# The scan of the RWKV heads: one series of batches over all four head pairs instead of four series

## The chip, the cores and the metric

One core of a Trainium2 chip. Times are device microseconds (us) of one launch; lower is better. The kernel before took a median of 2058.11 us in 3 runs (2053.48 to 2059.82).

## The reference, cut to what matters

The kernel is a two-layer trunk over 512 latent tokens and 256 context tokens of width 1024. In the even layer half of the heads are RWKV-7 heads, scanned forwards and backwards over the tokens:

```python
def rwkv7_scan(f, d, s0, reverse):
    def step(state, inp):
        r_t, w_t, k_t, v_t, kk_t, a_t = inp
        sa = jnp.einsum('bhvk,bhk->bhv', state, -kk_t)
        state = (state * w_t[:, :, None, :] + sa[..., None] * (kk_t * a_t)[:, :, None, :]
                 + v_t[..., None] * k_t[:, :, None, :])
        return state, jnp.einsum('bhvk,bhk->bhv', state, r_t)
...
    _, yl_f = rwkv7_scan(fl, 0, s_cf, False)
    _, yl_b = rwkv7_scan(fl, 1, s_cb, True)
    out_lat = rwkv7_output(fl, yl_f + yl_b, prm, pa_lat.dtype)
```

`rwkv7_prepare` computes r, k, v, the decay w, the rate a and the normalised key kk; `rwkv7_output` normalises y by head, adds a bonus term and gates it. The rest of the trunk (attention, MLP, adaLN modulation) isn't changed.

## The kernel before, in words

The eight RWKV heads are four pairs; a pair fills the 128 partitions. Tokens are cut into 12 chunks of 64 for each direction, and three chunks (`NB`) make a batch, so a pair has four batches.

**The prep** of a pair (`prep`) has four parts, with marks between them. Up to FRONT it makes the normalised key, the decays and rates (`wide` tiles at L405, L415, L865). Up to READY it makes the factors AR, BK and the chunk matrices XI (L903 to L948; L917 multiplies them on PE, L918 masks them on VectorE). The matrices then go through DRAM (`nscr`, L925 and L928) into another layout, N. Up to MERGE VectorE inverts the 32x32 blocks in 31 steps of two instructions (L954, L955), and the result goes back through DRAM (`xscr`, `tscr`, L959 to L967) into XI and `xw`. Behind MERGE the blocks are merged into 64x64 inverses: L974 and L982, two `wide` tiles each.

**The scan** of a pair (`chunks`) has seven stages for a batch: `factors` (transposes), `masked`, `own`, `solved` (multiplies by XI, L1077), `local` (L1089), `passed` (L1015) and three `step`s, which carry the state from chunk to chunk. Each batch's last stages are interleaved with the next batch's first ones, within one pair: a pair begins and ends with stages that have no partner. `mix_out` finishes a pair's output y.

**Who is handed out when.** These are Python generators; the trace is the order in which they are advanced. For each pair the main loop (L1488 to L1551) takes one stage of the scan a turn, 37 turns in all, and after each turn advances a background generator `behind` by 1.8 yields (RATE3) and the modulation matmuls `ada` (L353) by 0.7 (RATE4). `behind` deals in turn from the next pair's prep up to MERGE, the previous pair's `mix_out`, and the prep of the pair after the next up to FRONT. When the scan of the pair is through, `rest` hands out what is left: the prep of the pair after the next up to READY, then the next pair's merge. Only then does the next pair's scan begin.

The Tile planner orders each engine's instructions from this trace: what is traced earlier has precedence. Almost every matmul stage of the scan, the prep and `mix_out` writes a tile from `wide()`, of which there are two (two PSUM banks each); `py`, `pd` and the modulation's tile are others, one buffer each. AR, BK, XI, `wc` and `kds` of even and odd pairs lie in two pools, one buffer each, so a pair's prep from FRONT on waits for the scan of the pair two before it; `kds` also for that pair's `mix_out` (L1190). SyncE (SP) issues nearly all transfers, in order, the modulation weights (L341, three buffers of 512 KB) among them.

Of the kernel before, what the change touches and what calls it, by code (L numbers as in the profile page):

```python
# [174 lines left out]
def trunk(ctx: ExitStack, tc: tile.TileContext, xT, cT, vec_d, wada, we, wo_in, wout, wf1, wf2, lw2_d, la2_d, lg2_d,  # L175
# [5 lines left out]
    def act(o, i, f=AF.Copy, **k):  # L181
        return S.activation(o, i, f, **k)  # L182

    def pool(name, bufs=1, **k):
        return tc.tile_pool(name=name, bufs=bufs, reuse_waits="tile", **k)
# [657 lines left out]
    def prep(p, R, rt, iv, sts, res):  # L843
# [102 lines left out]
            yield QUIET  # L946
        G.tensor_tensor(kds, kds, kd, op=ALU.add)
        stt(kds, kds, VV["rk"][:, p:p + 1], r, op0=ALU.mult, op1=ALU.mult)  # L948
        yield READY
        for s in range(31):  # L950
            a, b = s + 1, 31 - s
# [10 lines left out]
        for d in range(2):  # L962
# [2 lines left out]
                i0 = d * 48 + b * 24  # L965
                nc.sync.dma_start(xv[o:o + 32, :, 32 * b:32 * b + 32], xscr[p, i0:i0 + 24].rearrange("i s t -> s i t"))
            nc.sync.dma_start(w1[d * 64:d * 64 + 32].rearrange("s (i t) -> s i t", t=32), tscr[p, d * 48:d * 48 + 24].rearrange("i s t -> s i t"))  # L967
        res[p] = (AR, BK, XI, wc, kds)
        yield MERGE
        for q in range(2):  # L970
            pw = one()
# [14 lines left out]

    NB = 3

    def chunks(p, y, ct, pch, res):

# [5 lines left out]
        ch = (FWD, BWD)  # L998
        v = ct.tile([128, T], F32, name="v")
        nc.sync.dma_start(v, scr[3 + 3 * p + 2])  # L1000
        py = pch.tile([128, 2, 512], F32, name="py")
        pd = pch.tile([128, 128], F32, name="pd")
        yp = py[:, :, 0:384].rearrange("p h (c f) -> p h c f", f=64)
        B = [{} for _ in range(NCH // NB)]
        last = None
        env = {}
# [55 lines left out]
        def own(b):  # L1062

            AK, Z, XA = (B[b][x] for x in ("AK", "Z", "XA"))
            px = wide()[:, 0:NB * 128].rearrange("p (i h v) -> p i h v", i=NB, h=2)
            for i in range(NB):
                for h, d in HD:
                    PE.matmul(px[half(d), i, h], AK[half(1 - d), h, i], Z[half(1 - d), i, d, h], start=True, stop=True)
            act(XA[:, :, :, 0:64], px)
# [12 lines left out]
        def local(b):  # L1082

            BT, Z = B[b]["BT"], B[b]["Z"]
            pn = wide()[:, 0:NB * 128].rearrange("p (i d v) -> p i d v", i=NB, d=2)
            for i in range(NB):
                for d in range(2):
                    for h in range(2):
                        PE.matmul(pn[half(h), i, d], BT[:, h, d * NB + i, 0:64], Z[:, i, d, h], start=True, stop=True)  # L1089
            N = B[b]["N"] = ct.tile([128, NB, 2, 64], F32, name="Nb", bufs=2)  # L1090
            act(N, pn)
            for i in range(NB):
                for h in range(2):
                    for d in range(2):
                        c = ch[d][NB * b + i]
                        first = not b and not i
                        o, x, y_ = yp[half(c % 2), h, c // 2], BT[:, h, d * NB + i, 64:128], Z[:, i, d, h]
                        if first:
                            env["y"] = PE.matmul(o, x, y_, start=True, stop=False)
                        else:  # L1100
                            with tc.issue_after(env["y"].ins):
                                PE.matmul(o, x, y_, start=False, stop=False)
# [17 lines left out]
        def step(b, i):  # L1120
            nonlocal X
            s = NB * b + i
            N = B[b]["N"][:, i]
            if not s:
                X = N
                return
            MQ, St = B[b]["MQ"], X
            if s < NCH - 1:
                for d in range(2):
                    for h in range(2):  # L1130
                        PE.matmul(pd[half(h), half(d)], MQ[half(h), d, i, 0:64], St[half(h), d], start=True, stop=True)
                X = ct.tile([128, 2, 64], F32, name="x", bufs=2)
                tt(X, pd.rearrange("p (d v) -> p d v", d=2), N, op=ALU.add)
            for d in range(2):
                c = ch[d][s]
                for h in range(2):
                    with tc.issue_after(env["y"].ins):
                        PE.matmul(yp[half(c % 2), h, c // 2], MQ[half(h), d, i, 64:128], St[half(h), d], start=False, stop=s == NCH - 1)

        nb = NCH // NB  # L1140
        for b in range(nb + 1):
            if b < nb:
                factors(b)
                yield
            if b:
                local(b - 1)
                yield
            if b < nb:
                masked(b)
                yield  # L1150
            if b:
                passed(b - 1)
                yield
            if b < nb:
                own(b)
                yield
            if b:
                step(b - 1, 0)
                yield
            if b < nb:  # L1160
                solved(b)
                yield
            if b:
                for i in range(1, NB):
                    step(b - 1, i)
                    yield
        act(y.rearrange("p c (h f) -> p h c f", h=2), yp)
        yield

    def centred(y):  # L1170

# [99 lines left out]
    def until(g, mark):  # L1271
        for t in g:
            if t == mark:
                return
            yield t

    def front(p):

        if p < 4:
            preps[p] = prep(p, R, rt, iv, sts, res)  # L1280
            yield from until(preps[p], FRONT)
# [188 lines left out]
    with ExitStack() as p2:  # L1470
# [10 lines left out]
            if t != QUIET:  # L1481
                next(ag, None)
        gate = mix_gate(tl)
        for t in until(preps[1], READY):
            next(ag, None)
        for t in preps[0]:
            next(ag, None)
        for p in range(4):  # L1488
            cg, n = chunks(p, y, ct, pch, res), 0

            def turns(*gs):
                gs = list(gs)
                while gs:
                    for g in list(gs):
                        t = next(g, gs)
                        if t is gs:
                            gs.remove(g)
                        else:
                            yield t

            def behind():
                def out():
                    return mix_out(p - 1, y, gate, tl, res) if p else iter(())
                if p < 3:
                    yield from turns(until(preps[p + 1], MERGE), out(), front(p + 2))
                else:
                    yield from out()
                    for x in mixs[::-1]:
                        x.close()
                    p3w["W"] = ffstream(p3w["x"].enter_context(pool("wp3")), 0)  # L1510
                    m0 = p3w["m0"] = p3w["m"].enter_context(pool("m0"))
                    p3w["last"] = m0.tile([128, T], F32, name="last")
                    yield from bonus(3, tl, res, gate, p3w["last"])
                    mh = m0.tile([128, KT, 256], F32R, name="mh")
                    ml = m0.tile([128, KT, 256], F32R, name="ml")
                    p3w["mh"] = mh, ml
                    for j in range(8):
                        for _ in range(3):
                            yield
                        p3w["W"].ahead(j + 1)  # L1520
                        if j in (5, 6):
                            a, b = ((4, 8), (0, 3))[j - 5]
                            if a:
                                mr = m0.tile([128, 4, 256], F32, name="mr")
                            else:
                                mr = tl.tile([128, T], F32, name="t", bufs=2).rearrange("p (k t) -> p k t", k=3)
                            nc.sync.dma_start(mr, mixd[a:b, :, 0:256].rearrange("k p t -> p k t"))
                            split(mh[:, a:b], ml[:, a:b], mr)
            bg = behind()
            due = [0.0, 0.0]  # L1530
            t = None
            for _ in cg:
                n += 1
                due[0] += RATE3
                due[1] += RATE4
                while due[0] >= 1:
                    due[0] -= 1
                    next(bg, None)
                while due[1] >= 1:
                    due[1] -= 1  # L1540
                    next(ag, None)
            def rest():
                if p < 2:
                    yield from until(preps[p + 2], READY)
                if p < 3:
                    yield from preps[p + 1]
            for t in itertools.chain(bg, rest()):
                due[1] += RATE5
                while due[1] >= 1:
                    due[1] -= 1  # L1550
                    next(ag, None)  # L1551
        for _ in ag:
            pass
        end = mix_last(3, y, tl, p3w["last"], p3w["gate"], mk)
# [336 lines left out]
```

## Time and profile before

| | us |
|---|---|
| profiled execution | 2055.19 |
| its span | 2053.4 |
| PE matmul busy | 1932.7 (94% of the span) |
| PE weight load busy | 1633.5 (80%) |
| VectorE busy | 1124.7 (55%) |
| ScalarE busy | 817.0 (40%) |
| GpSimd busy | 122.2 (6%) |
| mean granted clock of TensorE | 0.971 of full speed |

In the chain of waits that ended last PE has 63% of the span, VectorE 7%, ScalarE 3%, DMA 2%. A stretch of the trace is given from the start of the span. In rows of instructions the columns are: start, length in us, engine, line and operation, written tile and read tiles, shape, how many; in brackets the engine's idle time just before and what ended it. A name like PE L1077 means the instruction of line 1077 on that engine. A matmul in full 32-bit precision shows as two records.

### The profile page before, as it was taken

The numbers are of one execution on the slowest core, as the hardware profiler recorded it, in microseconds if no ns is written. First come the engines' busy times: TensorE is split into PE (matmuls) and PEld (weight loads), VectorE is DVE, ScalarE is ACT, GpSimd is POOL, SyncE is SP. The second block draws the span as 40 slices with busy tenths as digits, with TensorE's granted clock in tenths as the row PEclk, the third lists the DMA queues.
The fourth block names the chain that finished last, engine by engine and source line by source line (L and its number), as shares of the span: only waits on it lengthen the run. The fifth ranks groups of instructions, "written<-read, shape, count | busy, mean of one in ns | idle before, by whom it ended". The sixth has DMA issues, their size and how long they took to land.

```text
span 2053.4 us, 38620 instructions
## 1 busy us (share of the span) xinstructions
PE 1932.7 (94%) x16412; PEld 1633.5 (80%) x16412; DVE 1124.7 (55%) x1999; ACT 817.0 (40%) x1531; POOL 122.2 (6%) x149
## 2 busy tenths in 40 slices
PE   6999988988888899999999999899999899999997
PEld 3878767666666897888888889898888798888887
DVE  6576477547464377233433345856575575444445
ACT  3466442534335244311322122435686645222332
POOL 1000011011100000000000000001021000000000
PEclk9999989999999999999999999999999999999998
DMA  7422334666634233211221021342111334322221
GB/s 309 149 65 78 108 109 129 209 195 207 207 126 145 71 112 132 73 61 42 83 72 62 32 83 42 103 151 68 51 39 37 123 102 166 102 83 82 97 88 42
DMA packets 112013, 217.47 MB, mean 106 GB/s; under 512 B 38496, under 2 KB 63968, under 8 KB 111328
## 3 DMA queue, kind: packets, MB, share of 16 engines
q1 hardware_dynamic: 96544, 191.66, 28.6%
q10 hardware_dynamic: 15296, 23.33, 3.2%
q8 instruction: 129, 2.11, 0.4%
q14 instruction: 44, 0.36, 0.1%
HBM read 184.29 MB, written 28.05 MB: 103 GB/s over the span
## 4 chain that ended last, share of the span: by engine, by line
PE 63%; DVE 7%; ACT 3%; issue 3%; DMA 2%; POOL 1%; POOLq 0%; ACTq 0%; DVEq 0%; SPq 0%
PE x L1588 45%; PE x L430 5%; PE ax L530 2%; PE ax L511 2%; PE b L1015 1%; PE b L493 1%; PE ad L353 1%; PE b L1077 1%; PE b L494 1%; DMA w_raw<-in_wada_dram 1%; DVE X L955 1%; DVE nacc L288 1%; ACT Z L182 1%; DVE pr L954 1%; POOL r L264 0%
## 5 line engine op out<-in xcount | busy, mean ns | idle before, releaser
L182 ACT ACTIVATE w_hi<-w_raw 128x1024 fp32r<-128x1024 f32 x183 | 192.3, 1058 | 484.1 <-PE x L1588 369.1
L225 DVE TENSOR_TENSOR w_lo<-w_raw,w_hi 128x1024 fp32r<-128x1024 f32 x181 | 220.8, 1223 | 194.6 <-ACT w_hi L182 193.0
L1588 PE MATMUL x<-fl,w_hi 128*128 128x256 f32 (+1 forms) x864 | 290.9, 338 | 3.9 <-DVE fl L1675 3.9
L1588 PE MATMUL x<-uh,w_hi 128*128 128x512 f32 (+1 forms) x864 | 286.7, 337 | 3.0 <-ACT uh L182 3.0
L1588 PE MATMUL x<-fh,w_lo 128*128 128x256 f32 (+1 forms) x864 | 289.4, 336 | 0.0
L1588 PE MATMUL x<-ul,w_hi 128*128 128x512 f32 (+1 forms) x864 | 287.9, 336 | 0.0
L1588 PE MATMUL x<-uh,w_lo 128*128 128x512 f32 (+1 forms) x864 | 287.6, 336 | 0.0
L1588 PE MATMUL x<-fh,w_hi 128*128 128x256 f32 (+1 forms) x864 | 286.9, 337 | 0.0
L1602 DVE TENSOR_TENSOR oa<-x,oa 128x512 f32<-128x512 f32 (+1 forms) x184 | 103.1, 563 | 207.9 <-PE x L1588 207.0
L430 PE MATMUL x<-uh,w_hi 128*128 128x256 f32 (+1 forms) x560 | 190.2, 340 | 1.6 <-ACT po L182 1.3
L430 PE MATMUL x<-uh,w_lo 128*128 128x256 f32 (+1 forms) x560 | 189.1, 338 | 0.0
L430 PE MATMUL x<-ul,w_hi 128*128 128x256 f32 (+1 forms) x560 | 188.5, 337 | 0.0
L1588 PEld LDWEIGHTS x<-fl,w_hi 128*128 128x128 f32 x864 | 164.3, 190 | 22.0 <-DVE fl L1675 4.3
L1588 PEld LDWEIGHTS x<-uh,w_hi 128*128 128x128 f32 x864 | 161.8, 189 | 21.1 <-ACT uh L182 3.9
L1588 PEld LDWEIGHTS x<-fh,w_lo 128*128 128x128 f32 x864 | 164.1, 190 | 17.9
L1588 PEld LDWEIGHTS x<-fh,w_hi 128*128 128x128 f32 x864 | 162.1, 190 | 20.0 <-ACT fh L182 2.5
L1588 PEld LDWEIGHTS x<-ul,w_hi 128*128 128x128 f32 x864 | 162.8, 189 | 17.7
L1588 PEld LDWEIGHTS x<-uh,w_lo 128*128 128x128 f32 x864 | 162.8, 189 | 17.6
L430 PEld LDWEIGHTS x<-uh,w_hi 128*128 128x128 f32 x560 | 107.5, 192 | 12.5 <-issue 2.7
L430 PEld LDWEIGHTS x<-uh,w_lo 128*128 128x128 f32 x560 | 107.7, 192 | 9.4 <-issue 1.2
L430 PEld LDWEIGHTS x<-ul,w_hi 128*128 128x128 f32 x560 | 107.8, 192 | 9.2 <-issue 1.3
L1674 DVE TENSOR_TENSOR rl<-rl 128x512 f32<-128x512 f32 (+1 forms) x108 | 59.3, 550 | 77.7 <-ACT fh L182 77.5
(304 smaller groups left out, 3398.7 us busy)
## 6 DMA issues: line engine op xcount, KB each, us to landing
w_raw<-in_wf_dram SPq DMA_DIRECT2D x128, 512.0 KB
w_raw<-in_wada_dram SPq DMA_DIRECT2D x96, 512.0 KB
w_raw<-in_we_dram SPq DMA_DIRECT2D x21, 512.0 KB
w_raw<-in_wo_in_dram SPq DMA_DIRECT2D x18, 512.0 KB
w_raw<-in_wout_dram SPq DMA_DIRECT2D x16, 512.0 KB
hsc<-h ACTq DMA_DIRECT2D x8, 1024.0 KB
scr<-po ACTq DMA_DIRECT2D x21, 384.0 KB
h<-hsc SPq DMA_DIRECT2D x7, 1024.0 KB
```

Source lines behind the costliest of these rows:

```text
L182: return S.activation(o, i, f, **k)
L225: eng.tensor_tensor(o_lo, x, o_hi.bitcast(F32), op=ALU.subtract)
L288: V.tensor_reduce(acc, sq.rearrange("p k t -> p t k"), axis=AX.X, op=ALU.add)
L353: PE.matmul(ps[o:o + 32, 0:256], si[:, 2 * kp + k, :], w[:, k, j * 256:(j + 1) * 256], start=kp == 0, stop=kp == 3)
L430: PE.matmul(ps[:, 0:b - a], x, y, start=j == 0, stop=j == len(pairs) - 1)
L493: PE.matmul(ps[:, off:off + n], qs, kh, start=True, stop=False)
L494: PE.matmul(ps[:, off:off + n], qs, kl, start=False, stop=True)
L511: PE.transpose(pt[:, (kb - k0) * 128:(kb - k0 + 1) * 128], P[:, kb * 128:(kb + 1) * 128], ident)
L530: PE.matmul(po[h * 64:h * 64 + 64, 0:128], v(h, k), pts[h][:, k], start=k == 0, stop=k == n - 1)
L1588: PE.matmul(o, a, b, start=n == 0, stop=n == len(pairs) - 1)
L1602: tt(oa[:, m, tok], ps, oa[:, m, tok], op=ALU.add)
L1674: tt(r, r, r, op=ALU.mult)
```

## The change

The four scans become one. `chunks` is split: `stages` holds the stages of a pair, and `batches` runs 16 batches in one series, so that the stages of a pair's first batch stand between those of the last batch of the pair ahead. `pd` is allocated in each step and `py` in the first `local` of a pair. Ahead of `solved` of a pair's first batch `batches` yields MERGE; there the main loop hands out what is left of `behind`, and starts the next one. `behind(p)` now hands out, in this order: the prep of pair p + 1 up to READY; then, dealt in turn, its inverse up to MERGE, `mix_out` of pair p - 1 (once its y is written) and the prep of pair p + 2 up to FRONT; then the merge of pair p + 1. `res[p]` is set ahead of READY. Before the scan only the merge of pair 0 is handed out, no longer the prep of pair 1 up to READY.

```diff
+    def batches(y, ct, pch, res, done_y):
         nb = NCH // NB
-        for b in range(nb + 1):
...
+        pairs[0] = stages(0, y, ct, pch, res, done_y)
+        for g in range(4 * nb + 1):
+            new, old = g < 4 * nb, 0 < g
+            work = [new and (FACTORS, g), old and (LOCAL, g - 1), new and (MASKED, g), old and (PASSED, g - 1), new and (OWN, g),
+                      old and (STEP, g - 1, 0), new and (SOLVED, g), old and (STEP, g - 1, 1), old and (STEP, g - 1, 2)]
+            for w in filter(None, work):
+                if w[0] == SOLVED and not g % nb:
+                    yield MERGE
+                f, b = of(w[1], w[0])
+                f(b, *w[2:])
                 yield
...
-        for t in until(preps[1], READY):
-            next(ag, None)
         for t in preps[0]:
             next(ag, None)
...
+        def behind(p):
+            if p < 3:
+                yield from until(preps[p + 1], READY)
+                yield from turns(until(preps[p + 1], MERGE), outputs(p - 1), front(p + 2))
+                yield from preps[p + 1]
+                return
...
+        for t in batches(y, ct, pch, res, done_y):
+            if t == MERGE:
+                for _ in bg:
+                    modulation(RATE5)
+                bg, p = behind(p), p + 1
+                continue
+            modulation(RATE4)
+            due[0] += RATE3
+            while due[0] >= 1:
+                due[0] -= 1
+                next(bg, None)
```

## Rows read from the trace of the kernel before

**Rows 1.** Timeline, PE: first L917, first merge, each pair's first `solved` (L1077)

```profile
348.81 0.69 PE L917 MATMUL b<-ar,bk 64*64 64x64 f32 x8 [2.40 <-DVE po L1429]
...
357.05 1.99 PE L974 MATMUL b<-xw,XI 32*32 32x32 f32 x96
...
372.53 1.53 PE L1077 MATMUL b<-XA,XI 64*64 64x128 f32 x24 [0.59 <-ACT XA L182]
...
467.52 1.53 PE L1077 MATMUL b<-XA,XI 64*64 64x128 f32 x24
...
568.77 1.53 PE L1077 MATMUL b<-XA,XI 64*64 64x128 f32 x24
...
640.49 1.53 PE L1077 MATMUL b<-XA,XI 64*64 64x128 f32 x24 [0.59 <-ACT XA L182]
```

**Rows 2.** Busy times by stretch (instructions), granted clock, DMA share, GB/s

```profile
core 0: us, PE busy (x) PEld busy (x) DVE busy (x) ACT busy (x) POOL busy (x), PEclk, DMA share, GB/s
346.00:372.50 26.50, 19.25 (x445) 14.62 (x443) 15.80 (x23) 10.17 (x22) 5.16 (x5) 0.68 0.68 198
372.50:467.50 95.00, 85.78 (x1630) 59.44 (x1630) 54.28 (x125) 38.29 (x73) 8.94 (x10) 0.96 0.66 205
467.50:568.80 101.30, 88.09 (x1599) 62.50 (x1598) 58.86 (x127) 38.82 (x73) 13.01 (x12) 0.92 0.63 202
568.80:640.50 71.70, 62.65 (x1309) 48.69 (x1308) 44.48 (x104) 26.54 (x54) 7.73 (x8) 0.93 0.37 110
640.50:691.40 50.90, 43.21 (x919) 35.71 (x919) 24.16 (x32) 25.38 (x43) 1.75 (x2) 1.00 0.35 120
```

**Rows 3.** Timeline, PE: the prep's L405 and the scan's L1089

```profile
470.96 0.49 PE L1040 MATMUL b<-con,vr 128*128 128x128 f32 x3
...
478.23 2.67 PE L405 MATMUL b<-con,t 128*128 128x2 f32 x12 [1.26 <-ACT t L182]
...
480.83 1.55 PE L1089 MATMUL b<-Z,BT 128*64 128x64 f32 x24
```

**Rows 4.** Timeline, PE: last L917 of pair 2, first merge of pair 1

```profile
447.72 0.69 PE L917 MATMUL b<-ar,bk 64*64 64x64 f32 x30
448.34 0.24 PE L974 MATMUL b<-xw,XI 32*32 32x32 f32 x2
```

**Rows 5.** Timeline, DVE: last L918 and first L954, pairs 2 and 3

```profile
448.47 0.69 DVE L918 TENSOR_TENSOR XI<-b,con 128x512 f32<-128x512 f32 x1 [0.50 <-PE b L917]
...
474.66 0.18 DVE L954 TENSOR_TENSOR pr<-X,N 96x31 f32<-96x31 f32 x1
...
550.31 0.68 DVE L918 TENSOR_TENSOR XI<-b,con 128x512 f32<-128x512 f32 x1
...
577.81 0.18 DVE L954 TENSOR_TENSOR pr<-X,N 96x31 f32<-96x31 f32 x1
```

**Rows 6.** Timeline, SP: issues of pairs 2 and 3 (nscr; xscr, last xw)

```profile
460.33 3.86 SPq L925 DMA_DIRECT2D nscr<-XI  x4
...
510.06 0.34 SPq L959 DMA_DIRECT2D xscr<-X  x1
...
520.56 0.53 SPq L967 DMA_DIRECT2D xw<-tscr  x1
...
609.94 0.33 SPq L959 DMA_DIRECT2D xscr<-X  x1
...
617.76 0.53 SPq L967 DMA_DIRECT2D xw<-tscr  x1
```

**Rows 7.** Timeline, PE: bulk of pair 3's merge

```profile
625.51 1.70 PE L974 MATMUL b<-xw,XI 32*32 32x32 f32 x92
...
627.51 2.49 PE L982 MATMUL b<-XI,xw 32*32 32x32 f32 x96 [0.30 <-ACT xw L182]
```

**Rows 8.** Groups by line, 363 to 700 us: xcount | busy us, mean ns

```profile
L353 PE MATMUL ad<-w_raw,si 128*32 128x256 f32 x572 | 48.8, 409 | 7.1 <-DMA w_raw<-in_wada_dram 5.7 <-DVE mod L364 1.5
...
L955 DVE TENSOR_TENSOR X<-X,pr 96x31 f32<-96x31 f32 (+15 forms) x93 | 31.6, 340 | 2.5
```

**Rows 9.** Busy times, 380 to 430 us, columns as in rows 2

```profile
380.00:430.00 50.00, 46.90 (x861) 32.35 (x859) 37.22 (x92) 22.15 (x39) 3.64 (x5) 1.00 0.79 250
```

## What is expected of it

> **What bounds the kernel now.** I read the page first, then the busy times by stretch, then the order of the instructions on TensorE (PE), the transfer queue of SyncE (SP) and VectorE (DVE), each over the scan. Whole kernel: PE, at 94%. The change touches only the scan, from 346 to 691 us. I cut it at the first L1077 of each pair (`solved` of its first batch), at 372.5, 467.5, 568.8 and 640.5 us [rows 1]; I call these points S0 to S3, the stretches from one to the next P0 to P2, and P3 the one from S3 to 691.4.
>
> In these stretches PE is busy 85.8 of 95.0, 88.1 of 101.3, 62.7 of 71.7 and 43.2 of 50.9 us; ahead of S0 it is busy 19.3 of 26.5 at a granted clock of 0.68 [rows 2]. DVE stays under 62% and ScalarE (ACT) under 50%. So PE leads, but some 46 us of 345 are holes, and the clock is below 1 where it is idle. That is what a continuous series of batches could fill.
>
> What fills a hole is decided by the order of the shared PSUM tiles. Nearly every stage writes one from `wide()`, and there are two. The traced order of their users is worked out from the generators: 37 turns a pair, 1.8 background yields a turn. PE took them in that order throughout. At 471 us, with `local` of batch 0 (L1089) right behind the prep's L405 in that order, L405 came only at 478.2, after its `k`, and L1089 after it, at 480.8 [rows 3]; between them PE had only work on other PSUM tiles (modulation, `py`). The merge of pair 1 (L974) came right behind the last L917 of pair 2 [rows 4], traced ahead of it. Ahead of S0 PE idled for 2.4 us before L917, with pair 0's merge and first batch behind it, and the merge began at 357.05 [rows 1]. So I read: a `wide` user whose data is late holds up every later one. The scan's stages can't pass it.
>
> **The change part by part.** *One series.* 4x37 = 148 turns become 144. Nine stages stand between neighbouring batches everywhere, also at the three seams. The instructions are the same ones; nothing gets cheaper by itself.
>
> *The start.* Pair 1's prep up to READY (three L917 tiles, 348.8 to 357.05) no longer stands ahead of pair 0's merge. The merge takes its place: 348.8 plus the unchanged 372.5 - 357.05 = 15.5 gives S0' = 364.3 instead of 372.5. Gain 8.2.
>
> *Where prep and merge now stand.* This is the part that decides. Before, a pair's READY part ran in the seam ahead of the period, its inverse (62 DVE instructions, L954 and L955) in the period, its merge after the last step. Now READY, inverse and merge of pair p+1 all lie within period p, which has 36 turns and 36x1.8 = 65 yields. READY takes 17, so its third L917 is traced 5 turns behind S. Inverse to MERGE takes 15 yields, dealt in turn with 12 of `front` (periods 0 and 1) and 7 of `mix_out` (periods 1 and 2). The merge's first tile is therefore yield 45, 52 and 40, which is turn 25, 29 and 22 of 36. It sits in the order of `wide` there, with 11, 7 and 14 turns of scan behind it, whether its data has come or not.
>
> *How long its data takes.* From the end of the last L918 to the issue of the last `xw` transfer: pair 2, 449.2 to 521.1 = 71.9 us; pair 3, 551.0 to 618.3 = 67.3 [rows 5, 6]. Its pieces: 25.5 and 26.8 until the inverse starts (nscr out, N in), 35.4 and 32.1 for the inverse, 11.0 and 8.4 for xscr and back. The landing behind the last issue isn't shown; it lies between 0 and the 7.2 us until PE took the bulk of pair 3's L974, at 625.5 [rows 7]; I take 2. So c = 69 to 74 as measured.
>
> Shorter is possible: an L955 has 31.6 us for three pairs [rows 8], its multiply L954 the same shape, so the inverse alone on DVE is about 21 us. While PE stands before the merge, DVE has little else. Pair 2's nscr was issued 11.1 us after its data [rows 5, 6], behind a modulation load on SP, which need not recur. The transfers alone (460.3 to 474.7) took 14.3. The lower bound is 14.3+21+8.4 = 44. I take 63: 25 as both pairs had, 28 (between 21 and 35) for an inverse that has DVE half to itself, 8.4 and 2; nearer to the rows than to the bound, since only the inverse has a reason to shrink.
>
> *The periods.* From S to the last L918 there are five stages and three L917 at 0.7 [rows 4]: about 10 us, 12 in period 0, where the five hold no steps. After the merge begins, it takes 1.70+2.49 = 4.2 [rows 7], with its evictions 4.9, and the turns behind it go at P3's pace, 50.9/34 = 1.5 us. Period 0: 12+63+4.9+16.5 = 96.4 (95.0 before). Period 1: 10+63+4.9+10.5 = 88.4 (101.3). Period 2: 10+63+4.9+21 = 98.9 (71.7). Without the wait, period 2's scan would be at turn 22 after 22/37 of 71.7, 43 us, and would stand some 30 us for pair 3's merge, with only modulation to do. S3' = 364.3 + 283.7 = 648.0, against 640.5.
>
> *The last period.* Modulation was handed out at 0.7 a turn and 0.5 per yield between the pairs; the latter is nearly gone, so about 20 of its 101 yields are left for P3', where none ran before: 20% of 48.8 us of PE [rows 8] is 10 us, in 7.7 us of holes that can't all be used: +5. the transpose of pair 2's `mix_out` now stands two turns behind `y`, not four, and its data takes as long as before: two turns, +3. P3' = 59. The end is 707, against 691.4: +15.6.
>
> *At nothing:* a fresh `pd` per step (40 of them; the next product already waits for the read of the last one; 0 to 1 us), `py` allocated later (`act` of y was ahead of it before), the earlier load of `v` (it waits on SP for the same `vr` copies as before; what it could hold up there are modulation loads, 0 to 3 us), `y` and `kds` handed back in the same order. If the cover of `v` went, FACTORS of a seam would wait some 4 us.
>
> The profiled execution took 2055.19 us: 2053.4 of span and 1.8 around it. It lies 2.9 below the median of the runs, 2058.11, within their spread of 6.3. The sum: 2055.2+15.6 = 2070.8, on the scale of the median 2074.
>
> The granted clock fell to 0.68 where PE had holes ahead of S0 and stood at 1.00 in P3 [rows 2]. The Trainium skill (TensorE: Matmul & The Clock Gate, Part 1) says that the lower level is the default, and only activity releases it. By that rule the turns behind each wait would begin at 1.2 GHz, and the sum would rise by part of the 48 us that stand behind the three merges; I have not added it.
>
> **The rivals.** *Longer chain.* c stays at its measured 71.5 on average (nothing about the inverse shrinks): three times 8.5 more, +41, 2099. For it: both measured pairs. Against it: DVE was shared in both.
>
> *Faster: the seams are filled.* Place: the order of `wide`. If the merge's data is there when the scan reaches it (or the planner lets stages pass it), PE's work sets the time: 85.8x0.96, 88.1x0.92 and 62.7x0.93 full-clock us, the last with 7 more of modulation and L917, at 94% busy, as in the best stretch of the scan [rows 9]: 88+86+69 = 243, S3' = 607, the end 666: -25, 2033. It decides where c falls below 57.8, since each us of c is worth 3 and 15.6/3 = 5.2. For it: the lower bound of 44, and 46 us of holes. Against it: three places above where nothing passed. The Trainium skill (Perfetto Trace Analysis, Optimization Strategy) speaks for this rival: where the most-contended engine changes over time, it says, interleaving the regimes may help. By that rule the time would be this rival's; the rows show no reason that the interleaved order keeps the merge off the path.
>
> *No change.* c comes to 56 to 60: what the start and period 1 gain (8 and 13), period 2 and the end give back: 2058.
>
> **How the numbers follow.** A measurement of this kernel tells about 0.3%, 6.2 us, from no change. Forecast (c 60 to 68, +6 to +31, 2064 to 2089): 0.42. Longer chain: 0.13. No change: 0.18. Faster: 0.27. Slower is 0.55. The range, 2030 to 2098, leaves out about half of the longer chain and 0.4 of the fast case, 0.18 in all; the forecast's own is 2064 to 2089.
>
> **What would show it.** Right: PE standing with only modulation ahead of an L974 in periods 0 and 2, some 10 to 30 us in the latter; S0' near 364; period 2 longer than 71.7 and period 1 shorter than 101.3; the wait before L974 released by the `xw` transfers; some L353 in the last stretch. Wrong: L974 running at once when it is reached, or scan stages with `wide` tiles between the standing merge and its data; all three periods under 90; no wait at the merge and a time near 2033.

## The result, and the profile after

The changed kernel took a median of 2091.2 us in 4 runs (2086.2 to 2095.1), beside 2056.35 for the kernel before (4 runs): ratio 1.0167, 95% interval 1.0138 to 1.0196. The profiled execution has a span of 2084.4 us instead of 2053.4, and all of these 31 us come from the scan: it ends 31.6 us later, at 723.0 instead of 691.4.

Timeline of PE in the changed kernel, the first `solved` of each pair (L1074 there) as in [rows 1]:

```profile
361.75 1.53 PE L1074 MATMUL b<-XA,XI 64*64 64x128 f32 x24
...
454.38 0.43 PE L1074 MATMUL b<-XA,XI 64*64 64x128 f32 x2
...
556.98 0.43 PE L1074 MATMUL b<-XA,XI 64*64 64x128 f32 x2
...
658.16 1.48 PE L1074 MATMUL b<-XA,XI 64*64 64x128 f32 x24
```

Busy times of the changed kernel by stretch, cut at these points, columns as in [rows 2]:

```profile
346.00:361.80 15.80, 12.98 (x351) 9.01 (x350) 14.64 (x20) 9.85 (x22) 6.58 (x5) 1.00 0.82 279
361.80:454.40 92.60, 76.50 (x1462) 55.27 (x1461) 45.55 (x107) 34.40 (x65) 7.78 (x9) 0.85 0.49 146
454.40:557.00 102.60, 80.98 (x1521) 58.64 (x1521) 57.30 (x124) 37.18 (x70) 13.21 (x12) 0.88 0.45 134
557.00:658.20 101.20, 79.62 (x1515) 58.77 (x1514) 48.34 (x115) 27.75 (x60) 8.02 (x8) 0.81 0.55 165
658.20:723.00 64.80, 56.70 (x1062) 43.16 (x1054) 30.00 (x47) 27.71 (x48) 3.56 (x3) 0.92 0.50 166
```

| us | S0 | P0 | P1 | P2 | S3 | P3 | end |
|---|---|---|---|---|---|---|---|
| before | 372.5 | 95.0 | 101.3 | 71.7 | 640.5 | 50.9 | 691.4 |
| predicted | 364.3 | 96.4 | 88.4 | 98.9 | 648.0 | 59.0 | 707.0 |
| after | 361.8 | 92.6 | 102.6 | 101.2 | 658.2 | 64.8 | 723.0 |

In each of the three periods PE comes to a stand with only modulation to do, until the `xw` transfers land. The timelines of PE and of ScalarE around the merge of pair 1, and of PE at those of pairs 2 and 3:

```profile
407.96 0.91 PE L1065 MATMUL b<-Z,AK 64*64 64x64 f32 x24
...
432.58 1.08 PE L353 MATMUL ad<-w_raw,si 128*32 128x256 f32 x8 [5.55 <-DMA w_raw<-in_wada_dram]
434.04 0.31 PE L974 MATMUL b<-xw,XI 32*32 32x32 f32 x2 [0.38 <-DMA xw<-tscr]
434.28 2.83 PE L1074 MATMUL b<-XA,XI 64*64 64x128 f32 x24
...
537.49 0.42 PE L974 MATMUL b<-xw,XI 32*32 32x32 f32 x4 [0.59 <-DMA xw<-tscr]
539.91 2.77 PE L974 MATMUL b<-xw,XI 32*32 32x32 f32 x92 [2.00 <-DMA xw<-tscr]
...
626.88 0.31 PE L974 MATMUL b<-xw,XI 32*32 32x32 f32 x2 [0.88 <-DMA xw<-tscr]
627.12 1.55 PE L1086 MATMUL b<-Z,BT 128*64 128x64 f32 x24
```

```profile
408.92 0.49 ACT L182 ACTIVATE XA<-b 128x384 f32<-128x384 f32 x1 [2.79 <-PE b L1065]
```

`solved` of pair 0's last batch (L1074) had its data at 409.4, when XA was written. It ran at 434.28, right behind the merge's first products, and the scan behind it later still. Busy times in the changed kernel, stands and what came behind them:

```profile
414.40:434.00 19.60, 9.68 (x72) 3.49 (x72) 9.54 (x32) 0.77 (x2) 1.10 (x2) 0.56 0.92 258
434.00:447.00 13.00, 11.82 (x249) 9.90 (x250) 0.00 (x0) 6.01 (x12) 0.00 (x0) 0.63 0.41 129
...
524.60:537.40 12.80, 5.31 (x48) 2.27 (x47) 2.39 (x10) 0.38 (x1) 1.10 (x2) 0.68 0.87 226
537.40:549.00 11.60, 8.89 (x169) 6.93 (x171) 0.00 (x0) 3.90 (x8) 0.16 (x1) 0.50 0.43 145
...
601.60:626.80 25.20, 11.86 (x100) 4.31 (x100) 12.74 (x41) 1.37 (x5) 0.00 (x0) 0.69 0.86 250
...
626.80:645.00 18.20, 15.80 (x326) 13.48 (x328) 1.51 (x2) 5.40 (x10) 0.00 (x0) 0.50 0.39 122
```

The stands are some 20, 13 and 25 us long. Behind each, PE is busy again, 11.8 of 13.0, 8.9 of 11.6 and 15.8 of 18.2 us, but at a granted clock of 0.50 to 0.63.

### The profile page after: what moved, and what is told of

Read it like the earlier page. It is cut to its first block, busy times and chain, and to the rows that moved or that the text cites. A ratio compares the mean times of both kernels' runs of the same rounds, so it can differ in the third digit from the quotient of the medians.

```text
span 2084.4 us, 38591 instructions
## 1 busy us (share of the span) xinstructions
PE 1940.7 (93%) x16412; PEld 1637.6 (79%) x16412; DVE 1122.3 (54%) x1999; ACT 815.4 (39%) x1531; POOL 124.9 (6%) x149
## 4 chain that ended last, share of the span: by engine, by line
PE 77%; DVE 9%; issue 5%; ACT 4%; DMA 3%; POOL 2%; SPq 0%; POOLq 0%; ACTq 0%; DVEq 0%
PE x L1593 45%; PE x L430 11%; PE ax L530 3%; PE ax L511 2%; PE b L493 2%; PE ad L353 1%; PE b L494 1%; POOL r L264 1%; PE b L1012 1%; DVE X L956 1%; PE b L1074 1%; PE b L865 1%; DVE pr L955 1%; DMA tscr<-N 1%; DMA xw<-tscr 1%
```

## The experiments

The first five ask what the place of the merge and the length of its chain are worth, the others where modulation and the chain's transfers belong. Ratios are to the kernel before; differences in us between other kernels are those of the spans of their profiled executions.

**Merge handed out last.**

```diff
             if p < 3:
...
-                yield from preps[p + 1]
                 return
...
             if t == MERGE:
-                for _ in bg:
+                for _ in itertools.chain(bg, preps[p]):
                     modulation(RATE5)
```

> The changed kernel, with the merge of a pair handed out at MERGE, right ahead of the solved that needs it, and not in the middle of the period. Theory (the merge holds the order of the wide tiles): the 11, 7 and 14 turns behind the merge now run while its data is on the way. A period is then a + c + merge: 12.0+65.8+4.9 = 83, 13.7+71.8+4.9 = 90 and 13.4+58.9+4.9 = 77 us, against 92.7, 102.6 and 101.2 now, 46 us less in all: about 2045 us, 2035 to 2065. Rival (the period is set by the chain to the merge and by thinner filling work alone, wherever the merge stands; the stand would only move to the end of the period): 2085 to 2097.

Measured: 2043.96 us, ratio 0.9952 (0.9935 to 0.9970): 0.5% faster than the kernel before, little but clear of the noise, and 44 us faster than the changed one. Timeline of PE in it, pair 0's last `solved`, the merge of pair 1 and what follows, and below it the busy times of P0 to P2:

```profile
413.55 2.83 PE L1074 MATMUL b<-XA,XI 64*64 64x128 f32 x24
...
441.72 2.76 PE L974 MATMUL b<-xw,XI 32*32 32x32 f32 x92 [2.31 <-DMA xw<-tscr]
...
446.96 0.47 PE L1074 MATMUL b<-XA,XI 64*64 64x128 f32 x1
```

```profile
362.50:447.00 84.50, 72.57 (x1474) 54.47 (x1473) 51.95 (x117) 35.10 (x67) 10.41 (x10) 0.90 0.51 146
447.00:537.50 90.50, 79.54 (x1542) 57.33 (x1540) 57.38 (x123) 38.16 (x73) 14.91 (x12) 0.91 0.56 169
537.50:614.20 76.70, 69.75 (x1504) 52.90 (x1500) 44.44 (x109) 25.58 (x55) 8.38 (x8) 0.95 0.64 192
```

The `solved` that stood until 434.3 now runs at 413.6. The periods are 84.5, 90.5 and 76.7 us where the theory had 83, 90 and 77; the rival's unchanged time is out. The turns behind the merge were the loss.

**The merge in another PSUM tile**, at its old place in the order.

```diff
         for q in range(2):
-            pw = one()
+            pw = mk()
...
```

(in both loops of the merge).

> The changed kernel with the four products of a merge in the modulation's PSUM tile instead of a wide tile; its place in the traced order is as before. Theory (order of the wide tiles): the stages behind the merge pass it, the modulation waits in their place; the same three periods as with the merge handed out last, 83, 90 and 77 us or the PE work of a period where that is more; 2040 to 2070 us, and no wait of 10 us or more ahead of L974 with scan stages behind it. Rival (what is traced earlier goes first, whatever tile it writes): PE stands at L974 as now, 2085 to 2097.

Measured: 2069.8 us, ratio 1.0080 (1.0053 to 1.0108): 16 us of the changed kernel's time come back (span 2068.4), where the merge at the end brought 44 (2040.1). Timeline of PE at pair 1's merge:

```profile
436.79 0.92 PE L1065 MATMUL b<-Z,AK 64*64 64x64 f32 x24 [0.64 <-DVE BT L1057]
...
443.31 0.31 PE L974 MATMUL ad<-xw,XI 32*32 32x32 f32 x2 [1.12 <-DMA xw<-tscr]
...
453.20 1.49 PE L982 MATMUL ad<-XI,xw 32*32 32x32 f32 x48
```

`own` of the next pair's first batch (L1065), traced behind the merge, ran ahead of it: the `wide` tile held the stages, not the place in the trace alone. The full gain isn't reached. The four products of a merge now share one tile and take from 443.3 to 454.7, 11 us, where with the merge last they took 8 (439.0 to 447.0). Against that kernel the way from S to the last L918 is 5 to 6 us longer in each period, and in P1 the chain behind it takes 74.4 us to the merge instead of 68.5. So P1 stayed at 101.8 us; what made its chain longer was not tested.

**The inverse first, not dealt in turn.**

```diff
-                yield from turns(until(preps[p + 1], MERGE), outputs(p - 1), front(p + 2))
+                yield from until(preps[p + 1], MERGE)
+                yield from turns(outputs(p - 1), front(p + 2))
                 yield from preps[p + 1]
```

> The changed kernel with the inverse of the next pair handed out alone, ahead of mix_out and of the prep up to FRONT, no longer dealt in turn with them. It shortens c in periods 0 and 1 (the inverse took 35.4 and 40.7 us, 21 of them its own on VectorE), by some 10 us each, and moves the merge forward to yield 32, turn 18 of 36 in every period. Theory (the wide order): what c loses, the turns behind the merge give back, 18 instead of 11, 7 and 14 at 1.5 us: periods 0 to 2 change by about 0, +6 and +6 us; 2085 to 2110. Rival (only the length of the chain counts, wherever the merge stands): 20 us less, near 2070.

Measured: 2099.7 us, ratio 1.0230 (1.0197 to 1.0263). The number fell in the theory's range, but not for its reason. The expectation misread its own edit: what was taken out of the deal still stands ahead of the merge, so the merge didn't move forward. And the inverse got longer, not shorter: 41.5, 44.6 and 32.2 us for 35.4, 40.7 and 29.2, 13 us in all, and the span is 12 us longer. Timeline of DVE in the middle of pair 1's:

```profile
408.10 1.76 DVE L877 TENSOR_TENSOR_SCAN ei<-scan,t 128x768 f32<-128x768 f32 x1
409.77 0.39 DVE L955 TENSOR_TENSOR pr<-X,N 96x256 f32<-96x256 f32 x1
410.09 0.95 DVE L1057 TENSOR_TENSOR BT<-b,con 128x768 f32<-128x768 f32 x1
410.95 0.41 DVE L956 TENSOR_TENSOR X<-X,pr 96x256 f32<-96x256 f32 x1
411.29 1.75 DVE L879 TENSOR_TENSOR_SCAN ei<-scan,t 128x768 f32<-128x768 f32 x1
```

Between two steps of the inverse a larger instruction is run, though the prep's L877 and L879 are traced behind all of it. A chain of dependent steps doesn't get an engine to itself by being traced first.

**Half an inverse.**

```diff
         for s in range(31):
...
-            tt(tv, X[0:96, 0:a, s:s + 1]...
-            tt(X[0:96, 0:a, s + 1:32], ...
+            if s < 16:
+                tt(tv, X[0:96, 0:a, s:s + 1]...
+                tt(X[0:96, 0:a, s + 1:32], ...
```

> The changed kernel with the last 15 of the 31 steps of each inverse left out (30 VectorE instructions a pair; the yields stay, so nothing moves in the traced order). In the changed kernel these ran while PE stood: 11, 14 and 14 us. Theory: each us of c is a us of its period as long as PE stands at the merge (stands of 20 to 25, 15 and 25 to 28 us), so 39 us less, about 2052, 2040 to 2065. Rival (the stands are only where work is missing, and PE work or the clock sets the time): less than 10 us, 2080 to 2091.

Measured: 2045.99 us, ratio 0.9972 (0.9955 to 0.9989). Timeline of PE, the first products of each merge (L976 there):

```profile
421.45 0.31 PE L976 MATMUL b<-xw,XI 32*32 32x32 f32 x2
...
510.91 0.24 PE L976 MATMUL b<-xw,XI 32*32 32x32 f32 x2
...
585.84 0.31 PE L976 MATMUL b<-xw,XI 32*32 32x32 f32 x2
```

From the last L918 to them it took 44.8, 55.1 and 43.8 us, where the changed kernel took 60.3, 69.4 and 56.5: 42 less. The periods are 80.1, 86.0 and 86.7 us, 44 less (12.5, 16.6 and 14.5). So, in sum, a us of the chain is worth a us of the periods, as the prediction had it. The rival is out. The expectation put the steps left out into PE's stands; in P1 of the changed kernel they ran from 507.5 to 526.2, and the stand began only at 524.5. That period fell no less: what counted was when the chain ended.

**Both: merge last and half an inverse.** The two edits above.

> The merge handed out last, and the last 15 of the 31 steps of each inverse left out: what the one series is worth where the chain holds up nothing. The chain alone would then give periods of 84-13, 90-13 and 77-13 us (the 13 us that c lost when the steps were left out alone), 2005. Theory (work then sets the periods; the prediction's faster rival put that work at 88, 86 and 69 us, 243 in all against 251.6 with the merge last): 2035, 2025 to 2042, and no stand at the merge. Rival (the chain still sets them): 2000 to 2015.

Measured: 2027.12 us, ratio 0.9870 (0.9852 to 0.9889), in the theory's range. PE at the merge of pair 1, which no longer waits for `xw` (nor do those of pairs 2 and 3), and the busy times of P0 to P2:

```profile
430.16 0.24 PE L976 MATMUL b<-xw,XI 32*32 32x32 f32 x2 [0.59 <-ACT XA L182]
```

```profile
362.40:439.80 77.40, 71.19 (x1462) 53.77 (x1462) 41.52 (x83) 34.50 (x66) 6.84 (x9) 0.94 0.46 139
439.80:523.20 83.40, 77.44 (x1534) 56.76 (x1530) 46.88 (x93) 36.73 (x71) 14.35 (x12) 0.95 0.64 192
523.20:595.00 71.80, 65.84 (x1486) 49.85 (x1483) 34.92 (x79) 25.84 (x56) 8.07 (x8) 0.97 0.66 194
```

PE is now busy 92% of the three periods. They sum to 232.6 us; the faster rival of the prediction had put them at 243 and the time at 2033. This is what one series gives where the chain holds nothing up, with 15 steps of each inverse, and so some of DVE's work, left out.

**Modulation faster**, so that none is left for P3, in the changed kernel.

```diff
-RATE1, RATE2, RATE3, RATE4, RATE5 = 3.0, 1.5, 1.8, 0.7, 0.5
+RATE1, RATE2, RATE3, RATE4, RATE5 = 3.0, 1.5, 1.8, 0.88, 0.5
```

> The changed kernel with modulation handed out at 0.88 a turn instead of 0.7, so that none of it is left for the last stretch, where the trace of the changed kernel has 96 of its matmul records, 8.9 us of PE. Theory (the last stretch is PE's, the three before it have stands that take this work at no cost): 9 us less, about 2082, 2078 to 2088. Rival (it was hidden in the last stretch's holes): 2088 to 2095.

Measured: 2089.56 us, ratio 1.0183 (1.0158 to 1.0208): no gain, a miss. The time lies in the rival's range, but not for its reason alone: P3 did fall, from 64.8 to 60.0, and has no L353 left, so the term is worth 4.8 us, not 8.9. P0 and P1 took 3 us each for it, P2 gave back 2.6, and the start came 4.1 us later.

**The same rate with the merge last** (0.88), and a lower one (0.6).

> The kernel with the merge handed out last, and modulation at 0.88 a turn. Its stands ahead of the merge are only some 4 us in period 0, so the 9 us that leave the last stretch come back in part: about 2039, 2034 to 2044. If the periods are still the chain's alone, all 9 are gained: 2035. If they are work alone by now, none: 2044.

> The merge handed out last, and modulation at 0.6 a turn instead of 0.7 (at 0.88 the second and third period grew by 6 and 10 us and the last stretch lost 8). Theory (the periods are the chain's at 0.7 and can't get shorter, and what leaves them is added to the last stretch): 5 us slower, 2045 to 2053. Rival (modulation loads ahead of the chain's transfers on SyncE still lengthen the chain at 0.7): some us faster, 2036 to 2042.

Measured: 2052.22 us (0.9988, 0.9967 to 1.0010) and 2041.93 (0.9950, 0.9927 to 0.9973). At 0.88 P1 and P2 grew from 90.5 and 76.7 to 96.4 and 86.6, while P3 lost 7.3: the sum is worse than either theory had. At 0.6 the time lies in the rival's range, but the ratio is that of 0.7 (0.9952) within the intervals, so neither a gain nor a loss is shown. P0 and P1 got 2.1 and 3.8 us shorter, P2 and P3 1.5 and 2.5 longer. So with the merge last modulation has no free room in P1 and P2: they grow with it.

**The chain's transfers on GpSimd**, with the merge last, at 0.7 and at 0.88 a turn.

```diff
-        nc.sync.dma_start(N[0:96], nscr[p])
+        nc.gpsimd.dma_start(N[0:96], nscr[p])
```

and so for nscr, xscr, tscr, XI and `xw`.

> The kernel with the merge handed out last, and with the chain's transfers (nscr out, N in, xscr and tscr out, XI and xw in) issued from GpSimd instead of SyncE, where modulation loads stood between them: nscr to the start of the inverse took 15.0, 17.3 and 17.5 us, the inverse's end to the last xw issue 9.0, 10.2 and 8.7. Theory (the chain sets the period, and these loads are part of it): N follows nscr at once, some 5 us less of c in each period, 8 to 15 us in all where the scan of the period does not end last: about 2034, 2028 to 2040. Rival (GpSimd has the vr and kds work of the scan behind these waits, so what the chain gains the scan loses): 2040 to 2060.

> Merge last, the chain's transfers on GpSimd and modulation at 0.88 a turn together. Theory: the shorter chain makes room and the rate uses the last stretch; the two add up to 2029, 2022 to 2038. Rival (with the chain shorter the periods are work, and moved modulation lengthens them by what it takes off the last stretch): as with the transfers moved alone.

Measured: 2090.87 us (1.0188, 1.0161 to 1.0215) and 2073.92 (1.0104, 1.0078 to 1.0129). The first is far slower than both theories allowed. The second is far slower than its theory, but 17 us faster than the first, which its rival had not expected either. Timeline of PE at the merge of pair 1, at 0.7, and from the view of the tile `xw` its transfers' times from issue to landing:

```profile
453.83 0.42 PE L974 MATMUL b<-xw,XI 32*32 32x32 f32 x4
...
461.58 1.08 PE L353 MATMUL ad<-w_raw,si 128*32 128x256 f32 x8 [1.71 <-DMA w_raw<-in_wada_dram]
...
464.17 2.77 PE L974 MATMUL b<-xw,XI 32*32 32x32 f32 x92
```

```profile
L968 POOL DMA_DIRECT2D xw<-tscr x2: 717/717/717, 440.8 to 442.9; - x2
...
DMA to landing us min/median/max: 7.7/8.9/10.2
```

The last `xw`, issued at 442.9, was there by 453.1 at the latest; from SyncE, with the merge last, it was issued at 437.1 and the bulk of the merge ran at 441.7. Here the bulk came only at 464.17. Ahead of it PE's order now holds modulation (L353), whose groups have weights of their own to wait for; PE is busy 6.9 us of the 10 from 454 to 464. In each period the bulk came 10 us behind the first products, where it was 1 to 3 with the transfers on SyncE, and the first products came 7 to 10 us later behind S: together these are the 48 us by which the periods grew. Only in P2 at 0.88 a turn does the bulk follow within 2.3 us, with no modulation between. So filling work that stands ahead of a late product in PE's order can become the wait.

## Why the prediction came out as it did

Slower was the likeliest case, and the mechanism was the predicted one, but its sizes came out in part by luck. The end missed by 16.0 us (723.0 against 707.0): S0 -2.5, P0 -3.8, P1 +14.2, P2 +2.3, P3 +5.8. On the scale of the runs 2091 lies in the range given, above the forecast's 2064 to 2089.

*The start* was right and a little small: S0 came 10.8 us earlier, not 8.2.

*The order of `wide`* was right: a stage with its data at hand stood 25 us behind the merge, another tile frees the stages, and the merge at the end of the order frees them all. The prediction's sign that scan stages should not run between the standing merge and its data holds for all three periods up to the merge's first products; behind these a scan stage ran ahead of the bulk in P0 (L1074) and P2 (L1086). Its step "where prep and merge now stand" is the loss: it put 48 us of turns behind the merges, and the kernel with the merge last is 44 us faster.

*a, c and the rest.* The three terms of each period, from S to the last L918, from there to the merge's first products, and the rest:

| us | a | c | rest |
|---|---|---|---|
| P0 | 12.0 for 12 | 60.3 for 63 | 20.3 for 21.4 |
| P1 | 13.7 for 10 | 69.4 for 63 | 19.5 for 15.4 |
| P2 | 13.4 for 10 | 56.5 for 63 | 31.3 for 25.9 |
| sum | 39.1 for 32 | 186.2 for 189 | 71.1 for 62.7 |

The average c is 62, inside the forecast's 60 to 68, and the time is above the forecast: the 12.7 us by which the three periods were put too short lie in a and in the rest. And c itself is right in sum only because two errors cancel, which is luck. Timelines of SP and DVE in P1, from S to the inverse's end:

```profile
468.13 3.21 SPq L925 DMA_DIRECT2D nscr<-XI  x4
...
480.19 0.34 SPq L849 DMA_DIRECT2D k<-scr  x1
480.71 0.33 SPq L928 DMA_DIRECT2D N<-nscr  x1
```

```profile
465.95 0.96 DVE L1204 TENSOR_TENSOR y<-y,r 128x768 f32<-128x768 f32 x1 [2.38 <-POOL r L264]
466.83 1.28 DVE L918 TENSOR_TENSOR XI<-b,con 128x512 f32<-128x512 f32 x2
...
485.45 0.18 DVE L955 TENSOR_TENSOR pr<-X,N 96x31 f32<-96x31 f32 x1
...
525.97 0.21 DVE L956 TENSOR_TENSOR X<-X,pr 96x31 f32<-96x31 f32 x1
```

The way to the inverse was put at 25 us, as before, and took 15.0, 17.3 and 17.5: nscr was issued as soon as its data was there, which the prediction had seen as possible. The term that failed is "28 for an inverse that has DVE half to itself", with its reason that only the inverse could shrink: it took 35.4, 40.7 and 29.2. While the scan runs, larger instructions of the scan and of the preps run between its steps (in all DVE is busy 57.3 us of P1); when PE stands, its steps mostly follow one another. Of the three inverses 9.7, 1.7 and 15.5 us lay in a stand, and the less of it did, the longer it took. In P1 the transfers behind it took 11.3 us to the first products and 13.7 to the bulk, which waited for the second `xw`, instead of 10.4.

The excess of a in P1 and P2 is a wait that the prediction left out. PE was through with L917 at 463.8, but the last two L918 began only at 466.83. Ahead of them on DVE stood L1204, of the previous pair's `mix_out`, which waited for GpSimd (2.38 us). P2 has the same rows 102.3 us later.

*The clock.* Ahead of the stands the granted clock was at its upper level, 2.4 GHz (1.00 from 385 to 410, 495 to 520 and 580 to 600 us). In the stands, where PE was busy 9.7 of 19.6, 5.3 of 12.8 and 11.9 of 25.2 us, it fell, to a mean of 0.56 to 0.69; 0.50 is the lower level, 1.2 GHz. The Trainium skill (TensorE: Matmul & The Clock Gate, Part 1) calls the lower level the default, which activity releases; the trace agrees, with 0.63, 0.50 and 0.50 in the stretches behind the three merges. There PE was busy 11.8, 8.9 and 15.8 us. By an estimate from these rows (busy time times what the granted clock lacks to 1.00) at most 4.4, 4.4 and 7.9 us of it would not have been needed at the upper level. The prediction named this term and didn't add it. It may be part of the rest of P1 and P2, 4.1 and 5.4 us over; in P0 it shows no excess, and no run took it by itself.

*P3* was 5.8 us over. The modulation left there was sized right (+5 predicted, 4.8 by the rate's run). The other term, +3 for `mix_out`, was too small: without modulation P3 is still 9 us above 50.9. Of these 3.3 are PE's busy time, at a granted clock of 0.94 instead of 1.00, and 5.8 its holes (13.5 for 7.7). As long is its wait in that run for y ahead of the transpose (L1208), 5.76 us; in the changed kernel it was 4.33, and the scan's next stage stood behind it:

```profile
670.86 1.51 PE L1208 MATMUL b<-con,y 128*128 128x128 f32 x6 [4.33 <-DVE y L1204]
672.30 0.92 PE L1049 MATMUL b<-ar,bk 64*64 64x64 f32 x24
```

No run took this stand away by itself.

*The rivals.* The longer chain came true in P1 alone, if c is taken to the merge's bulk (71.8 for 71.5). The faster rival failed for the reason that was given against it. With the merge last its time, 2033, is nearly reached at 2044, and passed at 2027 where the inverse is halved too. The Trainium skill (Perfetto Trace Analysis, Optimization Strategy) holds that interleaving unlike regimes may help; here the interleaved series cost 1.7% with the merge in its middle and gained 0.5% with it at its end.

## What to carry to other kernels

When work is dealt among the stages of a loop, place each part by when its data is there and by when its result is needed, not by when its turn comes. A late part that takes a shared buffer in order holds up everything behind it, and the price is the work behind it, here 7 to 14 stages in each period. Handing it out at its deadline costs no instruction, and was worth 44 us.

## What was not expected of the hardware

In the changed kernel and the one with the merge last, each with modulation at 0.88 a turn, PE stood ahead of pair 0's second L982 for 3.5 and 4.1 us, for nothing that the profile shows ("issue"), where at 0.7 a turn that stand was below 0.4 us in both. It moved the start by up to 4 us. At 0.6 a turn with the merge last PE stood 2.4 us in the same way ahead of pair 0's first L974, and S0 came 5.2 us later than at 0.7. The cause is open.
